# Six of eleven pairs by seven products in the first half's down projection, with one sum of weights made ahead in the MLP's halves

## The chip, the cores and the metric

The kernel runs on one core of a Trainium2 chip. The metric is the device time of one execution in microseconds (us); the figure for a kernel is the median of its runs.

## The reference

One layer of an encoder on 256 tokens of width 2048, in float32:

```python
h = rms_norm(x, attn_norm)
qa, ka, va, qb, kb, vb, ga, gb = split(h @ w_in)
ya = windowed_gqa(qa, ka, va, table, sink)          # 8 heads, 2 key heads, |i-j| <= 128
yb = dilated_attention(qb, kb, vb, table)           # 12 heads in 3 groups of (window, dilation)
merged = sigmoid(ga) * (ya @ w_branch_a) + sigmoid(gb) * (yb @ w_branch_b)
x = x + merged @ w_out
hf = rms_norm(x, ffn_norm)
g = dwconv_centred(hf @ w_ffn_gate, conv_w, conv_b) # width 3, D_FF = 5632
x = x + (gelu(g) * (hf @ w_ffn_up)) @ w_ffn_down
x = x + sigmoid(rms_norm(x, ple_norm) @ w_ple_gate) * (p @ w_ple_proj)
return rms_norm(x, final_norm)
```

The change lies in the down projection (`w_ffn_down`, 5632 x 2048), which is done in two halves of 2816 rows, and in the first product of `w_ple_gate`.

## The kernel before

**Products in three thirds.** A float32 product is made of three matmuls on values that are split into a high and a low part: high by high, high by low, low by high (`thirds`, L363 to L368). So each weight is split on the way: ScalarE (ACT) copies a slice to its high part, `uh` or `vh` (L265), and VectorE (DVE) subtracts that from the slice to get the low part, `ul` or `vl` (L266).

**Pieces, units and rings.** Weights come as pieces of 1 MB (128 x 2048 float32) through SyncE's DMA queue into three `raw` buffers (`load`, L242). `produce` (L248) makes one unit of a piece, 512 or 1024 columns wide, in a ring of six units (`u`) or, for sums of weights, of two (`v`). TensorE (PE) uses units in the order in which they are made.

**Stages.** A: queries, keys, values and attention. B0 to B3: the gates, each followed by the branch projections `ba` and `bb`. D0 and D1: `w_out`, two column halves. E0: gate and up projections of the first half of the MLP, job by job (a job is one block of 128 columns of `w_ffn_gate` or `w_ffn_up`); F00 and F01: the down projection's part that belongs to it, for the two halves of the columns. E1, F10, F11 are the same for the second half. Then pp, G0, G2, G3 (`w_ple_gate`) and the last norm.

**Pairs.** In B, D, F and G0 a piece is a 2 x 2 block of quarters, 512 columns each, that is multiplied by a pair of activation rows (`quad_stage`, L373). A string gives the kind of each pair: `DOWN = "SsSsSsSsSss"` for each F stage. A pair "s" takes eight products (24 matmuls of 128 x 512); a pair "S" takes seven (21 matmuls) of sums, M1 to M7. For that it needs sums of weights, which `produce` makes in place in `raw` on DVE (L258: 1024 columns, L259 and L260: 512 each) ahead of the two `v` units, and sums of activations, which `sums_of` makes (L833). Each product adds up in a PSUM bank of its own, M1 to M7. At the last pair, which is always an "s", the row sums (`row_sums`, L806: L813 on ACT, L814 to L817 on DVE) read M1, M6, M7 and M5, and `residual` (L914) adds all to x (L927, L929). In B the banks M7 and M5 are also used by `bb`, whose last reads are L910.

**What sets the order.** Work of DVE and ACT is attached to places of a stage (`at`, `run_due`); a scheduler then sets the order in each engine's queue, in which an engine works strictly in sequence.

Of the kernel before, what the change touches and what calls it, by code (L numbers as in the profile page):

```python
# [10 lines left out]
F32 = mybir.dt.float32  # L11
# [5 lines left out]
P = 128  # L17
# [78 lines left out]
DOWN = "SsSsSsSsSss"  # L96
# [14 lines left out]
def _pieces():  # L111
# [29 lines left out]
    for half in range(2):  # L141
        names = {"g": "w_ffn_gate", "u": "w_ffn_up"}
        jobs = [(names[kind], f) for kind, f in _ffn(half)]
        joint = 0 if half else JOINT
        e = [(name, k, f) for k in range(KC) for name, f in jobs[:joint]]
        e += [(name, k, f) for name, f in jobs[joint:] for k in range(KC)]
        blocks("E%d" % half, e)
        for s in range(2):
            quads("F%d%d" % (half, s), ("w_ffn_down", 2 * s * WIDE), ("w_ffn_down", (2 * s + 1) * WIDE),
                  DOWN, half * FHALF)  # L150
# [4 lines left out]
    quads("G0", ("w_ple_gate", 0), ("w_ple_gate", WIDE), ALT)  # L155
# [9 lines left out]
def _unit_list():  # L165

    units, of = [], []
    for p, (kind, _) in enumerate(_PIECES):
        if p == 0:
            cuts = [("n", a * P, b * P) for a, b in ((0, 1), (1, 4), (4, 7), (7, 11), (11, PIECE))]  # L170
        elif kind == "S":
            cuts = [("n", 0, WIDE), ("n", 2 * WIDE, 4 * WIDE), ("T13", 0, 2 * WIDE), ("T24", 2 * WIDE, 4 * WIDE)]
        else:
            cuts = [("n", 0, 2 * WIDE), ("n", 2 * WIDE, 4 * WIDE)]
        of.append(list(range(len(units), len(units) + len(cuts))))
        units += [(p, *cut) for cut in cuts]
    return units, of
# [11 lines left out]
def _encoder(ctx: ExitStack, tc, xt, pt, xrow, cols, gainrow, table, onehot, mask, ident_in, wts, out):  # L189
# [22 lines left out]

    flat = big.tile([P, KC + KC * T], F32, name="x", tag="R1")
# [28 lines left out]
    def load(r, a=0, b=PIECE):  # L242
        if a == 0:
            raws[r] = wpool.tile([P, PIECE * P], F32, name="raw", bufs=3)
        nc.sync.dma_start(raws[r][:, a * P:b * P], wts[r][:, a * P:b * P])
        state["raw"] = r + 1

    def produce():  # L248
# [7 lines left out]
        if kind == "T13":  # L256
            q = [raw[:, i * WIDE:(i + 1) * WIDE] for i in range(4)]
            nc.vector.tensor_tensor(raw[:, :2 * WIDE], raw[:, WIDE:3 * WIDE], raw[:, :2 * WIDE], op=ALU.subtract)  # L258
            nc.vector.tensor_tensor(q[2], q[2], q[0], op=ALU.subtract)  # L259
            nc.vector.tensor_tensor(q[3], q[3], q[2], op=ALU.subtract)  # L260
        src = raw[:, a:b]
# [4 lines left out]
        nc.vector.tensor_tensor(lo, src, hi.bitcast(F32), op=ALU.subtract)  # L266
        made[u] = (hi, lo)
# [105 lines left out]
    def quad_stage(stage, moving, combos=None, tags=("M2", "M3", "M4", "P22")):  # L373
# [24 lines left out]
        for i, p in enumerate(pieces):  # L398
            kind = _PIECES[p][0]
            us = _UNITS_OF[p]  # L400
            a, b = moving(2 * i), moving(2 * i + 1)
# [8 lines left out]
            else:  # L410
                s = combos(i)
                sums = [(s[:, 0, e], s[:, 1, e]) for e in range(4)]
                for g, (name, stationary, u, c, gone) in enumerate((
                        ("M1", part(a, 0), 0, 0, 0), ("M7", sums[2], 2, 1, None), ("M5", sums[0], 2, 0, 2),
                        ("M6", sums[1], 3, 0, None), ("M4", part(b, 1), 3, 1, 3),
                        ("M2", part(b, 0), 1, 1, None), ("M3", sums[3], 1, 0, 1))):
# [190 lines left out]

    def view(a, offset, *dims):
        return bass.AP(tensor=a.tensor, offset=a.offset + offset, ap=[a.ap[0], *([step, n] for step, n in dims)])
# [223 lines left out]
    def sums_of(u, tag):  # L833
# [8 lines left out]
        s = tok.tile([P, 2, 4, P], FR, name="S", tag="S%d" % tag)  # L842
# [4 lines left out]
    combos = {}  # L847
# [113 lines left out]
    def activation_row(k):  # L961
        k %= FHALF
        return held["act"][1][k - 16] if 16 <= k < 20 else held["act"][k // 20 * 2][:, k - k // 20 * 20, :]
# [4 lines left out]
    def mlp(kind, n, acc):  # L968
# [21 lines left out]
        else:  # L990
# [8 lines left out]
            m = n % FHALF - 1  # L999
            if 16 <= m < 20:  # L1000
                for i in range(2):
                    halves(activation_row(m + i), u[:, i])
            else:
                i = m // 20 * 2
                d = held["act"][i][:, m - 10 * i:m - 10 * i + 2]
                nc.scalar.activation(d[:, :, :T], u, AF.Copy)
                nc.vector.tensor_tensor(d[:, :, T:], u, d[:, :, :T].bitcast(F32), op=ALU.subtract)
            pair = m // 2
            if DOWN[pair] == "S":
                combos["act", pair] = sums_of(u, pair // 2)  # L1010
# [13 lines left out]

    for half in range(2):
        held["act"] = [big.tile([P, 16, 2 * T], FR, name="act", tag="R1"),
                       [big.tile([P, 2 * T], FR, name="act1", tag="yb%d" % i) for i in range(4)],
                       held["tok"].tile([P, 2, 2 * T], FR, name="act2")]
# [9 lines left out]
        for kind, n in jobs[joint:]:  # L1038
            mlp(kind, n, product(stage, lambda k: hf[:, k, :], KC, "e"))
        if half:  # L1040
# [147 lines left out]
```

## Time and profile before

| | us |
|---|---|
| median of 3 runs | 1457.01 (1456.82 to 1458.02) |
| the profiled execution | 1457.09 |
| its span | 1455.3 |
| PE, DVE, ACT busy | 1444.2, 1196.8, 838.7 |
| B0 to D1, from 310 to 628 of the span | 318.0 |
| E0, 628 to 875.4 | 247.4 |
| F00 and F01, 875.4 to 987.5 | 112.1 |
| E1, 987.5 to 1232.5 | 245.0 |
| F10 and F11, 1232.5 to 1347 | 114.5 |
| pp, G0, G2, G3, end | 108.3 |

Times in the profile count from the start of the span; the granted clock of TensorE was 0.998. PE's rows are pipelined: the time that a row takes in a sequence is the distance to the next start. "PEld" is the loading of weights into TensorE. Behind an instruction stands in brackets how long its engine was idle before it, and what it waited for.

### The profile page before, as it was taken

How to read it: one execution, taken by the hardware profiler on the slowest of the kernel's cores; microseconds unless marked ns; L12 is line 12 of the kernel's file. 1: busy time of each engine (PE TensorE's matmuls, PEld its weight loads, DVE VectorE, ACT ScalarE, POOL GpSimd, SP SyncE). 2: the span in 40 equal slices, each digit the busy share in tenths (PEclk: the TensorE clock that was granted, in tenths of full speed). 3: DMA queues.
4: the chain of work that ended last, by engine and by line, in shares of the span. 5: the costliest groups of instructions: out<-in, count | busy, mean ns of one | idle time of the engine just before them, and what ended most of it. 6: DMA issues, size and time to landing. Idle time of an engine off the chain costs nothing.

```text
span 1455.3 us, 19303 instructions
## 1 busy us (share of the span) xinstructions
PE 1444.2 (99%) x7476; PEld 1234.3 (85%) x7476; DVE 1196.8 (82%) x1626; ACT 838.7 (58%) x1132; POOL 4.8 (0%) x9
## 2 busy tenths in 40 slices
PE   9999999999999999999999999999999999999997
PEld 8888888888888888888888888888888888888785
DVE  7677664679998989988787789987877778999994
ACT  7455544456555656666565565455655656565763
POOL 0000000000000000000000000000000000000000
PEclk9999999999999999999999999999999999999999
DMA  9653445535546456465555545465555554546462
GB/s 336 250 205 145 160 162 178 170 141 203 197 186 236 184 209 231 174 233 201 177 194 184 198 147 225 175 253 187 198 178 199 176 201 173 190 193 235 170 234 85
DMA packets 46455, 282.87 MB, mean 194 GB/s; under 512 B 4948, under 2 KB 9940, under 8 KB 14108
## 3 DMA queue, kind: packets, MB, share of 16 engines
q1 hardware_dynamic: 45644, 280.46, 52.8%
q8 instruction: 58, 0.95, 0.3%
q10 hardware_dynamic: 720, 1.19, 0.2%
q14 instruction: 33, 0.27, 0.1%
HBM read 279.49 MB, written 2.14 MB: 194 GB/s over the span
## 4 chain that ended last, share of the span: by engine, by line
PE 97%; DVE 1%; ACT 1%; issue 0%; DMA 0%; POOL 0%; POOLq 0%; DVEq 0%; SPq 0%; ACTq 0%
PE bank L309 29%; PE bank L316 15%; PE bank L366 14%; PE bank L367 14%; PE bank L368 14%; PE bank L355 2%; PE bank L357 2%; PE bank L293 2%; PE bank L356 2%; PE bank L294 1%; PE bank L861 1%; PE bank L678 0%; PE bank L626 0%; PE bank L625 0%; PE bank L624 0%
## 5 line engine op out<-in xcount | busy, mean ns | idle before, releaser
L265 ACT ACTIVATE uh<-raw 128x1024 fp32r<-128x1024 f32 (+2 forms) x519 | 523.1, 1015 | 394.0 <-PE bank L309 163.8
L266 DVE TENSOR_TENSOR ul<-raw,uh 128x1024 fp32r<-128x1024 f32 (+2 forms) x519 | 594.9, 1166 | 162.6 <-issue 81.0
L309 PE MATMUL bank<-hf,uh 128*128 128x512 f32 x1408 | 336.3, 391 | 0.0
L309 PEld LDWEIGHTS bank<-hf,uh 128*128 128x128 f32 x1408 | 258.9, 188 | 50.1
L316 PEld LDWEIGHTS bank<-hf,ul 128*128 128x128 f32 x1408 | 180.4, 191 | 6.7
L316 PE MATMUL bank<-hf,ul 128*128 128x256 f32 x1408 | 182.8, 283 | 0.0
L265 ACT ACTIVATE vh<-raw 128x1024 fp32r<-128x1024 f32 x92 | 97.0, 1056 | 42.4 <-DVE raw L258 22.9
L266 DVE TENSOR_TENSOR vl<-raw,vh 128x1024 fp32r<-128x1024 f32 x92 | 111.8, 1218 | 0.3
L309 PE MATMUL bank<-hs,uh 128*128 128x512 f32 x432 | 103.6, 392 | 0.0
L447 ACT ACTIVATE t<-bank 128x256 f32<-128x256 f32 x122 | 46.5, 383 | 97.4 <-PE bank L316 86.5
L309 PEld LDWEIGHTS bank<-hs,uh 128*128 128x128 f32 x432 | 79.5, 188 | 15.6
L366 PE MATMUL bank<-uh,act 128*128 128x512 f32 x232 | 90.4, 390 | 0.0
L367 PE MATMUL bank<-ul,act 128*128 128x512 f32 x232 | 90.4, 390 | 0.0
L368 PE MATMUL bank<-uh,act 128*128 128x512 f32 x232 | 90.2, 390 | 0.0
L366 PE MATMUL bank<-uh,hs 128*128 128x512 f32 x172 | 67.3, 391 | 0.0
L368 PE MATMUL bank<-uh,hs 128*128 128x512 f32 x172 | 67.2, 391 | 0.0
L367 PE MATMUL bank<-ul,hs 128*128 128x512 f32 x172 | 67.0, 389 | 0.0
L316 PE MATMUL bank<-hs,ul 128*128 128x256 f32 x432 | 56.6, 284 | 0.0
L258 DVE TENSOR_TENSOR raw<-raw 128x1024 f32<-128x1024 f32 x46 | 56.1, 1220 | 0.5
L316 PEld LDWEIGHTS bank<-hs,ul 128*128 128x128 f32 x432 | 54.5, 191 | 1.0
L367 PE MATMUL bank<-vl,S 128*128 128x512 f32 x138 | 54.0, 392 | 0.1
L366 PE MATMUL bank<-vh,S 128*128 128x512 f32 x138 | 54.1, 398 | 0.0
(242 smaller groups left out, 2229.4 us busy)
## 6 DMA issues: line engine op xcount, KB each, us to landing
raw<-in_wts SPq DMA_DIRECT2D x251, 1024.0 KB, 4.8
raw<-in_wts SPq DMA_DIRECT2D x12, 512.0 KB, 6.7
xr<-in_xrow SPq DMA_DIRECT2D x4, 512.0 KB, 8.2
x<-in_xt SPq DMA_DIRECT2D x13, 128.0 KB, 5.6
hb<-hold SPq DMA_DIRECT2D x3, 514.0 KB, 7.0
hb<-hold SPq DMA_DIRECT2D x2, 768.0 KB, 6.5
last<-in_gainrow SPq DMA_DIRECT2D x1, 1024.0 KB, 8.3
out<-xr SPq DMA_DIRECT2D x4, 256.0 KB, 2.6
```

The lines of the kernel that those rows point to most:

```text
L258: nc.vector.tensor_tensor(raw[:, :2 * WIDE], raw[:, WIDE:3 * WIDE], raw[:, :2 * WIDE], op=ALU.subtract)
L265: nc.scalar.activation(hi, src, AF.Copy)
L266: nc.vector.tensor_tensor(lo, src, hi.bitcast(F32), op=ALU.subtract)
L293: nc.tensor.matmul(acc, hi[:, w], m, start=first, stop=False, skip_group_check=True)
L309: nc.tensor.matmul(acc, weights(u)[0][:, o * P:(o + 1) * P], m, start=first, stop=False, skip_group_check=True)
L316: nc.tensor.matmul(acc[:, T:], weights(u)[1][:, o * P:(o + 1) * P], m[:, :T], start=False, stop=last, skip_group_check=True)
L355: nc.tensor.matmul(acc[:, :n * P], xh, hi, start=(k == 0), stop=False)
L356: nc.tensor.matmul(acc[:, :n * P], xh, lo, start=False, stop=False)
L366: nc.tensor.matmul(acc, sh, wh, start=first, stop=False)
L367: nc.tensor.matmul(acc, sh, wl, start=False, stop=False)
L368: nc.tensor.matmul(acc, sl, wh, start=False, stop=last)
L447: keep(nc.scalar.activation(t, acc[:, T:], AF.Copy, scale=scale))
```

## The change

The strings become `DOWN = ("ZZsZsZsZsZs", "ZsZsZsZsZss")`, one for each half of the MLP, so the first half's stages F00 and F01 have six pairs by seven products where they had five, and the second half's have five as before. G0's four "S" become "Z" as well; B and D keep "S".

A pair "Z" takes seven products as "S" does, in the order M1, M7, M6, M5, M4, M2, M3 and with other signs in its sums. Its quarters come in another order, and of its sums of weights one, q2 - q0 + q1, is made ahead, while the E stage of that half runs: `sum_ahead` loads three quarters' halves (128 x 3 x 256, 384 KB) through SP's queue into a buffer, DVE adds in two steps of 256 columns (L270, L271), and ACT's queue stores the sum (128 KB) in a DRAM tile `ahead`. Two such halves belong to a pair: 24 in all for the first half, 28 for the second with G0. Two buffers take turns ("act2" and "S4"). The load of a "Z" piece then takes 768 KB of weights (L253) and 256 KB of `ahead` (L254); the other two sums are made in place in two ops (L281: 512 columns, L282: 1024). The second of two "Z" in sequence makes its sums after its second unit. The activations of a "Z" pair are kept as the three quarters that M1, M2 and M4 use ("ends") and the four sums, where an "S" kept both whole rows and the sums.

```diff
-DOWN = "SsSsSsSsSss"
+DOWN = ("ZZsZsZsZsZs", "ZsZsZsZsZss")
+LASTS = 30
...
-            pieces.append((c, [(n0, a), (n1, a), (n1, b), (n0, b)]))
+            pieces.append((c, [(n1, a), (n0, a), (n1, b), (n0, b)] if c == "Z" else
+                           [(n0, a), (n1, a), (n1, b), (n0, b)]))
...
-    quads("G0", ("w_ple_gate", 0), ("w_ple_gate", WIDE), ALT)
+    quads("G0", ("w_ple_gate", 0), ("w_ple_gate", WIDE), ALT.replace("S", "Z"))
...
+        elif kind == "Z":
+            cuts = [("n", WIDE, 2 * WIDE), ("n", 2 * WIDE, 4 * WIDE), ("T21", 0, 2 * WIDE), ("T03", 2 * WIDE, 4 * WIDE)]
...
-        nc.sync.dma_start(raws[r][:, a * P:b * P], wts[r][:, a * P:b * P])
+        if _PIECES[r][0] == "Z":
+            nc.sync.dma_start(raws[r][:, WIDE:], wts[r][:, WIDE:])
+            nc.sync.dma_start(raws[r][:, :WIDE], ahead.pop(r))
+        else:
+            nc.sync.dma_start(raws[r][:, a * P:b * P], wts[r][:, a * P:b * P])
...
+    def sum_ahead(p, h, tag):
+        cols = slice(h * T, (h + 1) * T)
+        if h == 0:
+            ahead[p] = dram.tile([P, WIDE], F32, name="ahead%d" % p)
+        q = held["tok"].tile([P, 3, T], F32, name="ahead", tag=tag)
+        nc.sync.dma_start(q, wts[p][:, :3 * WIDE].rearrange("p (q c) -> p q c", c=WIDE)[:, :, cols])
+        def add():
+            nc.vector.tensor_tensor(q[:, 0], q[:, 2], q[:, 0], op=ALU.subtract)
+            nc.vector.tensor_tensor(q[:, 0], q[:, 0], q[:, 1], op=ALU.add)
+        def store():
+            nc.scalar.dma_start(ahead[p][:, cols], q[:, 0])
+        return add, store
+
+    def sums_of_weights(raw):
+        q = [raw[:, i * WIDE:(i + 1) * WIDE] for i in range(4)]
+        nc.vector.tensor_tensor(q[1], q[0], q[1], op=ALU.subtract)
+        nc.vector.tensor_tensor(raw[:, 2 * WIDE:], raw[:, 2 * WIDE:], view(q[0], 0, (0, 2), (1, WIDE)), op=ALU.subtract)
...
+        behind = _PIECES[p][0] == "Z" == _PIECES[p - 1][0]
+        if kind == "T21" and not behind:
+            sums_of_weights(raw)
...
+        if behind and u == _UNITS_OF[p][1]:
+            sums_of_weights(raw)
...
+                if kind == "S":
+                    todo = (("M1", m1, 0, 0, 0), ("M7", sums[2], 2, 1, None), ("M5", sums[0], 2, 0, 2),
+                            ("M6", sums[1], 3, 0, None), ("M4", m4, 3, 1, 3),
+                            ("M2", m2, 1, 1, None), ("M3", sums[3], 1, 0, 1))
+                else:
+                    todo = (("M1", m1, 0, 0, 0), ("M7", sums[2], 2, 1, None), ("M6", sums[1], 2, 0, 2),
+                            ("M5", sums[0], 3, 0, None), ("M4", m4, 3, 1, 3),
+                            ("M2", m2, 1, 1, None), ("M3", sums[3], 1, 0, 1))
...
+            x, y = place
+            for b, k, t0, t1 in ((0, 0, 0, P), (1, 1, 0, T)):
+                o = x[:, :, b:b + (t1 - t0) // P]
+                v = u[:, k, t0:t1].rearrange("p (b t) -> p b t", t=P)
+                nc.scalar.activation(o[:, 0], v, AF.Copy)
+                nc.vector.tensor_tensor(o[:, 1], v, o[:, 0].bitcast(F32), op=ALU.subtract)
+            combos["act", pair] = sums_of(u, None, y)
...
+        todo = [(p, h) for p in sevens(half) for h in range(2)]
+        for i, (kind, n) in enumerate(jobs[joint:]):
+            if len(stores) > 1:
+                stores.pop(0)()
+            for f in adds:
+                at((stage, 8), f)
+            del adds[:]
+            def ask():
+                if todo and i > 1 and (i % 2 == 0 or i < LASTS):
+                    add, store = sum_ahead(*todo.pop(0), ("act2", "S4")[i % 2])
+                    adds.append(add)
+                    stores.append(store)
+                else:
+                    stores.append(lambda: None)
+            at((stage, 9), ask)
             mlp(kind, n, product(stage, lambda k: hf[:, k, :], KC, "e"))
```

The scheduler moves some of this. On DVE the ten sums of the first half that use the "act2" buffer stand in B1 to D1 instead of E0. At the start of B2, where `bb` has just ended (L910 before, L956 now, reads its banks), DVE's rows before:

```order
L266 TENSOR_TENSOR vl_3913<-raw_3782,vh_3912 128x1024
L266 TENSOR_TENSOR ul_3947<-raw_3847,uh_3946 128x1024
L910 SCALAR_TENSOR_TENSOR c_3810<-c_3810,bank_3952 128x512
L912 TENSOR_TENSOR c_3810<-c_3810 128x512
L266 TENSOR_TENSOR ul_3975<-raw_3889,uh_3974 128x512
L910 SCALAR_TENSOR_TENSOR c_3811<-c_3811,bank_3953 128x512
L266 TENSOR_TENSOR ul_3985<-raw_3889,uh_3984 128x1024
```

and now, with an add in it:

```order
L305 TENSOR_TENSOR vl_3913<-raw_3782,vh_3912 128x1024
L305 TENSOR_TENSOR ul_3947<-raw_3847,uh_3946 128x1024
L956 SCALAR_TENSOR_TENSOR c_3810<-c_3810,bank_3952 128x512
L270 TENSOR_TENSOR ahead_6350<-ahead_6350 128x256
L305 TENSOR_TENSOR ul_3975<-raw_3889,uh_3974 128x512
L958 TENSOR_TENSOR c_3810<-c_3810 128x512
L956 SCALAR_TENSOR_TENSOR c_3811<-c_3811,bank_3953 128x512
L305 TENSOR_TENSOR ul_3985<-raw_3889,uh_3984 128x1024
```

One add of 256 columns stands between the two reads of `bb`'s banks.

At the border from F00 to F01 the rows of DVE before are these (`raw_8211` is F01's first pair, `c` the row sums, `xr` is x):

```order
L816 TENSOR_TENSOR c_8337<-bank_7957,c_8337 128x512
L266 TENSOR_TENSOR ul_8289<-raw_8211,uh_8288 128x1024
L266 TENSOR_TENSOR vl_8296<-raw_8211,vh_8295 128x1024
L259 TENSOR_TENSOR raw_8211<-raw_8211 128x512
L817 TENSOR_TENSOR c_8338<-bank_7957,c_8338 128x512
L260 TENSOR_TENSOR raw_8211<-raw_8211 128x512
L266 TENSOR_TENSOR ul_8330<-raw_8251,uh_8329 128x1024
L266 TENSOR_TENSOR ul_8334<-raw_8251,uh_8333 128x1024
L266 TENSOR_TENSOR vl_8300<-raw_8211,vh_8299 128x1024
L927 TENSOR_TENSOR xr_4918<-xr_4918,bank_7986 128x512
```

and now (`raw_8369` and `raw_8405` are F01's first and second pair, both "Z"; L859 to L862 are the row sums, L281 and L282 the sums of weights):

```order
L305 TENSOR_TENSOR vl_8478<-raw_8369,vh_8477 128x1024
L305 TENSOR_TENSOR ul_8495<-raw_8405,uh_8494 128x1024
L859 TENSOR_TENSOR c_8500<-bank_8102,c_8500 128x512
L282 TENSOR_TENSOR raw_8405<-raw_8405 128x1024
L860 TENSOR_TENSOR c_8501<-bank_8098,c_8500 128x512
L973 TENSOR_TENSOR xr_4918<-xr_4918,bank_8139 128x512
L861 TENSOR_TENSOR c_8500<-bank_8110,c_8500 128x512
L862 TENSOR_TENSOR c_8501<-bank_8110,c_8501 128x512
L973 TENSOR_TENSOR xr_4918<-xr_4918,bank_8143 128x512
L973 TENSOR_TENSOR xr_4918<-xr_4918,bank_8114 128x512
L975 TENSOR_TENSOR xr_4918<-xr_4918,c_8500 128x1024
L973 TENSOR_TENSOR xr_4918<-xr_4918,bank_8210 128x512
```

The row sums, which stood among the sums of the first pair, now stand behind the low parts of the first pair and around the second sum of the second.

PE's rows of F01's second "Z" now (`ends` and `S` are its activations, L407, L408 and L409 the three thirds):

```order
L407 MATMUL bank_8537<-uh_8484,ends_6211 128x512
L408 MATMUL bank_8537<-ul_8485,ends_6211 128x512
L409 MATMUL bank_8537<-uh_8484,ends_6211 128x512
L407 MATMUL bank_8541<-vh_8549,S_6212 128x512
L407 MATMUL bank_8545<-vh_8549,S_6212 128x512
L407 MATMUL bank_8582<-uh_8494,ends_6211 128x512
L408 MATMUL bank_8582<-ul_8495,ends_6211 128x512
L407 MATMUL bank_8553<-vh_8561,S_6212 128x512
L407 MATMUL bank_8557<-vh_8561,ends_6211 128x512
L409 MATMUL bank_8582<-uh_8494,ends_6211 128x512
L408 MATMUL bank_8541<-vl_8550,S_6212 128x512
L409 MATMUL bank_8541<-vh_8549,S_6212 128x512
```

The products with the high parts `vh` stand ahead of those with the low parts `vl` of the same units.

In E1, DVE's rows of one stretch before:

```order
L266 TENSOR_TENSOR ul_10069<-raw_9972,uh_10068 128x1024
L266 TENSOR_TENSOR ul_10081<-raw_9972,uh_10080 128x1024
L451 TENSOR_TENSOR gw_9990<-bank_10041,t_10084 128x256
L977 TENSOR_TENSOR gw_9990<-gw_9990,rms_5811 128x512
L981 SCALAR_TENSOR_TENSOR gw_9990<-gw_9990,cl_73 128x255
L983 SCALAR_TENSOR_TENSOR gw_9990<-gw_9990,cl_73 128x255
L981 SCALAR_TENSOR_TENSOR gw_9990<-gw_9990,cl_73 128x255
L266 TENSOR_TENSOR ul_10126<-raw_10019,uh_10125 128x1024
L983 SCALAR_TENSOR_TENSOR gw_9990<-gw_9990,cl_73 128x255
```

and now:

```order
L305 TENSOR_TENSOR ul_10129<-raw_10021,uh_10128 128x1024
L305 TENSOR_TENSOR ul_10141<-raw_10021,uh_10140 128x1024
L499 TENSOR_TENSOR gw_10039<-bank_10096,t_10144 128x256
L271 TENSOR_TENSOR ahead_10295<-ahead_10295 128x256
L1049 TENSOR_TENSOR gw_10039<-gw_10039,rms_5806 128x512
L270 TENSOR_TENSOR ahead_10348<-ahead_10348 128x256
L1053 SCALAR_TENSOR_TENSOR gw_10039<-gw_10039,cl_73 128x255
L271 TENSOR_TENSOR ahead_10348<-ahead_10348 128x256
L1055 SCALAR_TENSOR_TENSOR gw_10039<-gw_10039,cl_73 128x255
L1053 SCALAR_TENSOR_TENSOR gw_10039<-gw_10039,cl_73 128x255
L305 TENSOR_TENSOR ul_10191<-raw_10073,uh_10190 128x1024
```

Between the rows of the gate's convolution stand the two adds of one sum, and the second add of another.

More of the change, by code (lines that the diff above doesn't have):

```diff
@@ L412, in quad_stage @@
                 sums = [(s[:, 0, e], s[:, 1, e]) for e in range(4)]
[L413 to L416, printed above, removed]
+                m1, m2, m4 = (part(a, 0), part(b, 0), part(b, 1)) if (stage, i) not in ends else ends[stage, i]
+                if kind == "S":
[6 more added lines that the diff above has]
+                            ("M2", m2, 1, 1, None), ("M3", sums[3], 1, 0, 1))
+                for g, (name, stationary, u, c, gone) in enumerate(todo):
                     run_due(stage, i, g)
```

79 lines of the change are left out of this document (55 added, 24 removed).

## The prediction

> **What bounds the kernel now.** I read the page's busy times and chain first, then the table of stretches, then PE's own waits, and only then DVE's and ACT's.
>
> ```profile
> PE 1444.2 (99%) x7476; PEld 1234.3 (85%) x7476; DVE 1196.8 (82%) x1626; ACT 838.7 (58%) x1132; POOL 4.8 (0%) x9
> PE 97%; DVE 1%; ACT 1%; issue 0%; DMA 0%; POOL 0%; POOLq 0%; DVEq 0%; SPq 0%; ACTq 0%
> PE bank L226 <- DVE mhalf L221: 1.1, 1, 1.1
> PE bank L293 <- ACT uh L265: 0.2, 1, 0.2
> ```
>
> The chain that ended last is PE for 97% of the span, and the list of PE's waits holds 1.3 us. So an instruction less on PE is time won, and one less elsewhere is not, except where DVE is nearly as full as PE. The stretches show where that is (columns: window, length, busy time of PE, PEld, DVE, ACT, POOL, granted clock, DMA share, GB/s):
>
> ```profile
> 310.00:628.00 318.00, 317.99 (x1430) 261.05 (x1429) 299.38 (x370) 189.19 (x219) 0.00 (x0) 1.00 0.53 198
> 628.00:875.40 247.40, 247.40 (x1429) 218.55 (x1427) 195.24 (x289) 149.56 (x210) 0.71 (x1) 1.00 0.53 188
> 875.40:930.90 55.50, 55.50 (x246) 45.92 (x245) 51.96 (x58) 30.20 (x33) 0.00 (x0) 1.00 0.53 196
> 930.90:987.50 56.60, 56.60 (x251) 46.89 (x250) 50.92 (x55) 29.60 (x32) 0.00 (x0) 1.00 0.59 225
> 987.50:1232.50 245.00, 245.00 (x1411) 216.54 (x1410) 188.88 (x272) 144.09 (x196) 0.00 (x0) 1.00 0.52 186
> 1232.50:1347.00 114.50, 114.50 (x511) 94.42 (x510) 109.76 (x132) 66.38 (x79) 0.00 (x0) 1.00 0.57 211
> ```
>
> These are B0 to D1, E0, F00, F01, E1, and F10 with F11. In B to D and in the F stages DVE is busy for 90 to 96% of the time; in the E stages for 77 to 79%.
>
> **Step 1: two more pairs by seven products.** PE loses one product, three matmuls, in F00 and in F01. What a matmul costs in a row is the distance of starts, not its busy time:
>
> ```profile
> 931.60 0.39 PE L366 MATMUL bank<-vh,S 128*128 128x512 f32 x1
> 931.82 0.39 PE L367 MATMUL bank<-vl,S 128*128 128x512 f32 x1
> 932.05 0.39 PE L368 MATMUL bank<-vh,S 128*128 128x512 f32 x1
> 932.28 0.39 PE L366 MATMUL bank<-vh,S 128*128 128x512 f32 x1
> 932.96 0.39 PE L366 MATMUL bank<-vh,S 128*128 128x512 f32 x1
> ```
>
> Three matmuls take 0.68 us (931.60 to 932.28), so the six are 1.36 us: **-1.36**. A pair of eight products is 8 x 0.68 = 5.44 us on PE, one of seven 4.76.
>
> **Step 2: DVE in the pairs.** These rows price its work (columns: busy us, mean ns; starts follow 0.08 us less apart than that, as 424.85, 425.45 below show):
>
> ```profile
> L266 DVE TENSOR_TENSOR vl<-raw,vh 128x1024 fp32r<-128x1024 f32 x92 | 111.8, 1218 | 0.3
> L258 DVE TENSOR_TENSOR raw<-raw 128x1024 f32<-128x1024 f32 x46 | 56.1, 1220 | 0.5
> L266 DVE TENSOR_TENSOR ul<-raw,uh 128x512 fp32r<-128x512 f32 x47 | 32.3, 687 | 10.6 <-ACT uh L265 10.3
> L259 DVE TENSOR_TENSOR raw<-raw 128x512 f32<-128x512 f32 x46 | 31.5, 685 | 0.3
> L260 DVE TENSOR_TENSOR raw<-raw 128x512 f32<-128x512 f32 x46 | 31.5, 684 | 0.2
> L451 DVE TENSOR_TENSOR pair<-bank,t 128x256 f32<-128x256 f32 x44 | 18.4, 418 | 0.2 <-ACT t L447 0.2
> ```
>
> S made three sums of weights in place, 1.22 + 0.69 + 0.68 = 2.59 us; Z makes two (512 and 1024 wide), 1.90: 0.69 less a pair. A pair of eight products has two lo halves (2.44 us); a Z has one of 512 and three of 1024 (4.34) besides its sums, so it costs DVE 6.24, 3.8 more than "s". F00 and F01: 5 x -0.69 + 3.8 = +0.4 us of DVE each while PE gets 0.68 less, so DVE goes from 51.96 of 55.5 to about 52.4 of 54.8. F10 and F11 save 3.4 each, G0 2.8. None of this is on the path by itself, but two places in F have less cover.
>
> (a) F00 and F01 begin with two Z: 2 x 6.24 = 12.5 us of DVE against 9.5 of PE. The 3.0 us must be made ahead; the new PE order helps, since it does the second Z's hi products before its lo ones. I take 0; the other end is half the deficit, +1.5, if the ring of two v units keeps DVE from going ahead.
>
> (b) The border from F00 to F01. The last three products' banks are read by the row sums (L813 to L817), and F01's M7 and M5 need those banks:
>
> ```profile
> 924.46 0.68 DVE L259 TENSOR_TENSOR raw<-raw 128x512 f32<-128x512 f32 x1
> 925.06 0.68 DVE L817 TENSOR_TENSOR c<-bank,c 128x512 f32<-128x512 f32 x1
> ```
>
> The last row sum ends at 925.74, and M5 starts at 932.96 (the last row of the fence before): 7.2 us to spare, because two pairs "ss" end the stage. Now one "s" does, 5.44 us less: 1.8 us are left, and the new order sets the row sums behind the first Z's lo halves and among the second Z's sums. The sums start only after ACT's copy of M1 and behind two 1024 ops (2.28 us by start distance). 2.28 - 1.8 = about +0.5 us of wait: taken **+0.5**, ends 0 (they follow at once) and +2.5 (both ops and the 1024 sum of the second Z, 1.22, and a row sum, 0.68, all late). It replaces no wait that was there.
>
> **Step 3: sums made ahead.** 24 times for half 0 and 28 for half 1: a load of 384 KB on SP, two DVE ops of 256 columns (0.84 us), a store of 128 KB from ACT's queue, and later 256 KB of each Z's megabyte come from that store. In E this has cover:
>
> ```profile
> L266 DVE TENSOR_TENSOR ul<-raw,uh 128x1024 fp32r<-128x1024 f32 x87 | 104.3, 1221 | 42.8 <-issue 40.9 <-PE bank L316 1.9
> 701.93 3.65 PE bank L309 x16
> 705.59 1.91 PE bank L316 x16
> ```
>
> The first row is DVE's lo halves in E1 alone: DVE stood idle for 42.8 us before them, nearly all of it with a full ring of units ahead of PE. The adds of E1 are 28 x 0.84 = 23.4 us, so 19 us of slack remain; E0 gets the 14 that are not moved forward, 11.7 us. The other two rows are the chain in an E job: 3.65 + 1.91 = 5.56 us, two units of the ring of six, so a full ring is two jobs ahead, 11.1 us; a DVE that falls a microsecond or two behind inside a job is not seen by PE. I take 0. Price if the cover goes: in Rival 1.
>
> Ten of half 0's sums stand earlier, in B1 to D1, where DVE is the second bound: 10 x 0.84 = 8.4 us against 318.0 - 299.38 = 18.6 us of idle DVE. There the order matters; PE waits for DVE at the start of a B stage:
>
> ```profile
> 424.85 0.68 DVE L266 TENSOR_TENSOR ul<-raw,uh 128x512 fp32r<-128x512 f32 x1
> 425.45 0.68 DVE L910 SCALAR_TENSOR_TENSOR c<-c,bank 128x512 f32<-128x512 f32 x1
> 426.18 0.19 PEld L366 LDWEIGHTS bank<-vh,S 128*128 128x128 f32 x1 [0.26 <-DVE c L910]
> 607.84 0.19 PEld L366 LDWEIGHTS bank<-vh,S 128*128 128x128 f32 x1 [0.42 <-ACT vh L265]
> 620.53 0.19 PEld L367 LDWEIGHTS bank<-vl,S 128*128 128x128 f32 x1 [0.27 <-DVE vl L266]
> 1349.02 0.42 PEld L861 LDWEIGHTS bank<-ident,xr 128*128 128x128 f32 x4 [0.42 <-DVE xr L927]
> 1374.05 0.19 PEld L367 LDWEIGHTS bank<-vl,S 128*128 128x128 f32 x1 [0.51 <-DVE vl L266]
> ```
>
> At 426.18 PE waits for L910, DVE's last read of the bank that M5 takes over. An add of 0.42 us, 0.34 by start distance, now stands two ops before it, and likewise at the starts of B3 and D0. If nothing else moved that is 3 x 0.34 = +1.0; but the order now has other PE work ahead of M5 (transposes and products with ready weights, some 0.5 us), which covers most. Taken +0.2 for the three (0 to +1.0). D1 has two more waits (607.84 and 620.53); three adds in it and a new order on both engines: from -0.4 (both gone) to +1.3 (three times 0.42), taken 0, since the adds stand where DVE waits for ACT. E0's beginning needs D1's last work from DVE, up to 1.7 us (four adds) later; E0's first column blocks do not need it, so I take +0.1, with +1.0 as the far end. At 1374.05 in G0 PE waits 0.51 us from the end of one weight load to the next, of which some 0.25 is lost (a row's distance is 0.23); G0's sums are shorter by 0.69, so **-0.25**. At 1349.02, at F11's end, PE waits for DVE's last row of x (0.42); F11's DVE has less to do, but that row depends on the last product, so 0.
>
> **DMA.** The new transfers by their nearest rows (columns: KB, us to landing):
>
> ```profile
> raw<-in_wts SPq DMA_DIRECT2D x251, 1024.0 KB, 4.8
> raw<-in_wts SPq DMA_DIRECT2D x12, 512.0 KB, 6.7
> raw<-in_wts SPq DMA_DIRECT2D x1, 320.0 KB, 5.1
> xr<-in_xrow SPq DMA_DIRECT2D x4, 512.0 KB, 8.2
> out<-xr ACTq DMA_DIRECT2D x4, 256.0 KB, 2.9
> x<-in_xt ACTq DMA_DIRECT2D x1, 136.0 KB, 2.5
> ```
>
> A buffer of the sums is turned once in two jobs, 11.1 us: load 5.1, adds 0.84, store 2.5, together 8.4; with the slowest row, 8.2 + 0.84 + 2.9 = 11.9. At 5.1 nothing waits, and 5.1 is the row of nearest size. Traffic in E goes from 188 GB/s by 0.52 MB in 5.56 us, 94, to some 282, and DMA's share of 0.53 rises with it to about 0.8, so transfers get slower, which is Rival 1's ground. A Z's load is 768 + 256 KB where it was 1024; SP's queue has one more issue, and three raw buffers stand behind it: 0.
>
> The Trainium skill, page "DMA: Bandwidth & Descriptors", section "Anatomy of one DMA", gives a fixed 2.0 us and 436 KB per us beyond that; as an estimate from it the load of 384 KB would take 2.9 us and the store 2.3, a turn would be 6.0 us, and the sum would stay as it is. The same page, section "Bandwidth", has the rule to batch transfers to at least 1 MiB, which speaks against the change; the trace's 2.5 us for 136 KB lies near that estimate, while 5.1 us for 320 KB lies well above the 2.8 us that it would give.
>
> **Sum:** -1.36 + 0 + 0.5 + 0.2 + 0 + 0.1 - 0.25 = -0.8. The profiled execution took 1457.09 us (span 1455.3 and 1.8 around it), 0.08 above the median of the runs, 1457.01. So I forecast 1456.2, 0.06% less, which a measurement of this kernel can't tell from no change (some 0.2%, 2.9 us). With the ends of all terms: (a) +1.5, (b) 0 to +2.5, B starts 0 to +1.0, D1 -0.4 to +1.3, E0 0 to +1.0; a few of them together give 1455 to 1458.5.
>
> **Rivals.**
> 1. Slower: the turn of the sums' buffers limits E. Place: SP's queue in E1, where each 384 KB load stands ahead of a weight load and waits until the store from two jobs before has landed. It decides from a turn of over 11.1 us; at 11.9 each turn loses 0.8 us, half 1 has 14 turns of each buffer, 11 us, and with more traffic it would be more. The 11.1 us of the ring take the first part. For it speak DMA's share of 0.8 and the 8.2 us row, against it the 5.1 us row and that three raw buffers are loaded behind. Time: +4 to +10, 1461 to 1467. Chance 0.14.
> 2. The F stages become DVE's: at the "ZZ" starts and the border the ends of (a) twice and (b) come together, 3.0 + 2.5 - 1.36 - 0.35 = +3.8, or half of it. For it speaks 96% of DVE, against it the PE order that puts ready products first. 1457.5 to 1460.9. Chance 0.14.
> 3. Faster: DVE's relief takes PE's small waits away as well, G0's 0.25, D1's 1.0, the B starts' 0.3, F11's 0.4, and no new ones come: -1.36 - 1.95 = -3.3, 1453.7. For it: new orders everywhere. Against: the adds lie in just those stages. Chance 0.09.
> 4. It changes nothing at all, since another limit holds F: 1457.0. Against it stands PE's 55.50 of 55.50. It is not told from my forecast by the time, only by F's length; chance 0.03.
>
> The forecast has the remaining 0.60, with 1455.0 to 1457.8 as its own range. Faster by over 0.2% (below 1454.1) is most of Rival 3: 0.08. Slower (above 1459.9) is Rival 1 and a fifth of Rival 2: 0.17. The rest, 0.75, is within 0.2%. Left out are 0.07 below 1454.0 and about 0.12 above 1461.0.
>
> **What the profile after would show.** Step 1: six matmuls fewer on PE, F00 and F01 each 0.5 to 0.7 us shorter. (a) and (b): a wait of PE for DVE at the first M7 or M5 of F01, under 1 us. Step 3: E0 and E1 as long as before (247.4 and 245.0) with DVE 10 and 22 us fuller; longer E stages with SP waiting for the stores would make Rival 1 right. B2 to D0: waits for L956 (L910 now) of 0.1 to 0.4 us. I am wrong if E grows by more than a microsecond, or if F shrinks by more than 1.4.

## The result, and the profile after

The changed kernel takes 1474.2 us (median of 6 runs, 1472.93 to 1482.97) against 1456.95 (6 runs, 1456.75 to 1458.02): a ratio of 1.0128, 95% interval 1.0103 to 1.0152. It is 1.3% slower, where the forecast was 1456.2. The profiled execution has a span of 1475.0 us, 19.7 longer than before. Its page, in the lines that answer to those shown of before:

```profile
PE 1450.7 (98%) x7470; PEld 1236.7 (84%) x7470; DVE 1220.0 (83%) x1730; ACT 828.1 (56%) x1148; POOL 5.0 (0%) x9
PE 83%; DMA 7%; DVE 7%; issue 2%; ACT 1%; SPq 0%; POOLq 0%; POOL 0%; DVEq 0%; ACTq 0%
PE bank L350 23%; PE bank L407 12%; PE bank L409 12%; PE bank L408 12%; PE bank L357 12%; DMA ahead<-in_wts 4%; DVE ul L305 3%; DMA ahead<-ahead 3%; PE bank L396 2%; PE bank L398 2%; PE bank L397 2%; PE bank L334 2%; PE bank L335 1%; DMA raw<-in_wts 1%; PE bank L907 1%
```

PE has its six instructions less (7470 for 7476), but the chain that ended last is PE for only 83% of the span. Two transfers that did not exist before are in it by name: the load of a sum (`ahead<-in_wts`) and its store (`ahead<-ahead`). The stretches, cut where each stage begins on PE, show where (columns as before; B0 to D1, E0, F00 with F01, E1, the rest):

```profile
310.00:630.40 320.40, 318.60 (x1428) 260.69 (x1428) 304.88 (x391) 187.72 (x219) 0.00 (x0) 1.00 0.58 213
630.40:877.60 247.20, 247.20 (x1427) 218.33 (x1426) 202.69 (x322) 143.63 (x215) 0.81 (x1) 1.00 0.60 219
877.60:989.70 112.10, 112.10 (x494) 91.99 (x493) 104.25 (x114) 63.40 (x70) 0.00 (x0) 1.00 0.57 211
989.70:1253.10 263.40, 251.87 (x1410) 219.15 (x1410) 206.87 (x334) 137.57 (x201) 0.00 (x0) 0.99 0.65 230
1253.10:1475.00 221.90, 212.32 (x952) 175.06 (x950) 189.63 (x246) 127.79 (x175) 2.93 (x3) 0.98 0.51 186
```

Measured from the first matmul of each stage to that of the next, in both kernels:

| stage | before | after | difference |
|---|---|---|---|
| to the start of E0 | 627.24 | 630.40 | +3.16 |
| E0 | 247.10 | 247.20 | +0.10 |
| F00, F01 | 113.02 | 112.11 | -0.91 |
| E1 | 244.90 | 263.35 | +18.45 |
| F10 to the end | 223.04 | 221.98 | -1.06 |
| span | 1455.30 | 1475.04 | +19.74 |

So all but 3 us of the loss is in E1. The waits of E1, by engine, tell what PE stood behind (columns: us in total, times, longest):

```profile
PE bank L357 <- DVE ul L305: 11.1, 10, 3.2
DVE ahead L270 <- DMA ahead<-in_wts: 41.4, 14, 5.2
SPq L267 <- DMA ahead<-ahead: 108.8, 18, 10.4
```

PE waits for the low parts of weights; DVE, which makes them, stands at the first add of a sum (L270) 14 times and for 41.4 us until the sum's load has landed; and that load (L267) stands in SP's queue until the store of the sum that used the buffer before has landed. The chain of E1 between 1064 and 1083 us follows this back (columns: start, us, what):

```profile
1064.25 6.46 DMA ahead<-ahead
...
1070.76 2.91 DMA ahead<-in_wts
...
1073.76 0.43 DVE ahead L270
1074.19 0.10 DVE ahead L271
...
1074.55 4.55 DMA ahead<-ahead
...
1079.15 3.20 DMA ahead<-in_wts
```

A store takes 6.5 or 4.6 us, a load 2.9 or 3.2, and nothing lies between them but an add. The chain goes from one buffer to the other: the add that starts at 1073.76 belongs to one sum, and the second add of the sum before it, whose store starts at 1074.55, stands behind it in DVE's queue. DVE's rows at this place show both things, in the order in which DVE has them:

```profile
1069.16 0.41 DVE L270 TENSOR_TENSOR ahead<-ahead 128x256 f32<-128x256 f32 x1
1073.76 0.43 DVE L270 TENSOR_TENSOR ahead<-ahead 128x256 f32<-128x256 f32 x1 [4.20 <-DMA ahead<-in_wts]
1074.10 0.75 DVE L271 TENSOR_TENSOR ahead<-ahead 128x256 f32<-128x256 f32 x2
1074.77 2.35 DVE L305 TENSOR_TENSOR ul<-raw,uh 128x1024 fp32r<-128x1024 f32 x2
1077.04 0.42 DVE L499 TENSOR_TENSOR pair<-bank,t 128x256 f32<-128x256 f32 x1
1082.47 0.42 DVE L270 TENSOR_TENSOR ahead<-ahead 128x256 f32<-128x256 f32 x1 [5.01 <-DMA ahead<-in_wts]
```

The first two rows are the first adds of two sums, one in each buffer; the third row has the second adds of both; the last row is the next sum of the first buffer. Between the last add of the first sum and that row lie some 3 us of DVE's work, but a store and a load must pass there, some 8 us. DVE works in order, so it waits.

When PE's starts are set beside those of before, the first 67 us of E1 (to 1056) lose 0.1 us, although DVE waits 14.2 us for sums' loads in them. Then it loses 9.0 by 1093, 6.5 between 1111 and 1137, and 2.9 between 1148 and 1175, in steps. This fits a ring of units that stands full ahead of PE, pays for the first waits, and is empty after them.

Not all of the 18.45 us is waiting. Two stretches of 3.4 us each, within 2 us of the end of two of PE's longest waits, have a granted clock of 0.50 (columns as before):

```profile
1085.80:1089.10 3.30, 3.30 (x12) 2.81 (x11) 2.97 (x8) 2.30 (x4) 0.00 (x0) 0.50 0.79 276
1130.10:1133.40 3.30, 3.30 (x17) 3.24 (x16) 1.04 (x2) 3.12 (x5) 0.00 (x0) 0.50 0.48 160
```

In them PE's matmuls of 512 columns start 0.43 us apart, where 0.23 is their usual distance. These stretches cost 3.1 us of the 18.45, and the waits the other 15.3. Of the twelve profiles of this document, those of the changed kernel and of runs (2), (4) and (6) below have such stretches before the last 30 us; they are also the only ones in which, from 60 to 1440 us, two starts on PE lie 2.0 us or more apart. Run (1), with at most 1.4 us, has none. The six runs of the changed kernel have mean clocks of 0.992 to 0.997, and the longest of them has the lowest. So in these runs the lower clock goes with long waits of PE and adds to their price; what sets the limit was not tried.

### The profile page after: what moved, and what is told of

It reads as the page before. It is cut to its first block, busy times and chain, and to the rows that moved or that the text cites. A ratio compares the mean times of both kernels' runs of the same rounds, so it can differ in the third digit from the quotient of the medians.

```text
span 1475.0 us, 19731 instructions
## 1 busy us (share of the span) xinstructions
PE 1450.7 (98%) x7470; PEld 1236.7 (84%) x7470; DVE 1220.0 (83%) x1730; ACT 828.1 (56%) x1148; POOL 5.0 (0%) x9
## 4 chain that ended last, share of the span: by engine, by line
PE 83%; DMA 7%; DVE 7%; issue 2%; ACT 1%; SPq 0%; POOLq 0%; POOL 0%; DVEq 0%; ACTq 0%
PE bank L350 23%; PE bank L407 12%; PE bank L409 12%; PE bank L408 12%; PE bank L357 12%; DMA ahead<-in_wts 4%; DVE ul L305 3%; DMA ahead<-ahead 3%; PE bank L396 2%; PE bank L398 2%; PE bank L397 2%; PE bank L334 2%; PE bank L335 1%; DMA raw<-in_wts 1%; PE bank L907 1%
## 5 line engine op out<-in xcount | busy, mean ns | idle before, releaser
L357 PE MATMUL bank<-hf,ul 128*128 128x256 f32 x1408 | 187.3, 285 | 11.5 <-DVE ul L305 11.1
L304 ACT ACTIVATE vh<-raw 128x1024 fp32r<-128x1024 f32 x96 | 100.8, 1057 | 62.1 <-DVE raw L281 25.0
L305 DVE TENSOR_TENSOR vl<-raw,vh 128x1024 fp32r<-128x1024 f32 x96 | 116.1, 1218 | 0.9
L409 PE MATMUL bank<-uh,act 128*128 128x512 f32 x218 | 84.9, 390 | 0.0
L408 PE MATMUL bank<-ul,act 128*128 128x512 f32 x218 | 84.8, 389 | 0.0
L407 PE MATMUL bank<-uh,act 128*128 128x512 f32 x218 | 84.6, 389 | 0.0
L270 DVE TENSOR_TENSOR ahead<-ahead 128x256 f32<-128x256 f32 x52 | 21.8, 420 | 73.2 <-DMA ahead<-in_wts 69.2
L407 PE MATMUL bank<-uh,hs 128*128 128x512 f32 x172 | 67.4, 392 | 0.0
L408 PE MATMUL bank<-ul,hs 128*128 128x512 f32 x172 | 67.1, 390 | 0.0
L409 PE MATMUL bank<-uh,hs 128*128 128x512 f32 x172 | 67.0, 390 | 0.0
L408 PEld LDWEIGHTS bank<-ul,act 128*128 128x128 f32 x218 | 40.9, 188 | 8.6
L409 PEld LDWEIGHTS bank<-uh,act 128*128 128x128 f32 x218 | 40.9, 188 | 8.5
```

The source lines that it names most:

```text
L304: nc.scalar.activation(hi, src, AF.Copy)
L357: nc.tensor.matmul(acc[:, T:], weights(u)[1][:, o * P:(o + 1) * P], m[:, :T], start=False, stop=last, skip_group_check=True)
L407: nc.tensor.matmul(acc, sh, wh, start=first, stop=False)
L408: nc.tensor.matmul(acc, sh, wl, start=False, stop=False)
L409: nc.tensor.matmul(acc, sl, wh, start=False, stop=last)
```

## The experiments

Each starts from the changed kernel. Theory "order": the scheduler's dense rows on DVE. "Turn": two buffers are too few at any order. "Queue": SP, waiting for stores, holds the weights back. "Traffic": the added bytes. "Work": the added DVE time. E1's lengths below are from first matmul to first matmul, as in the table. Where no ratio is given, the kernel was run once.

**Adds tied to their place (1).** `keep` ties an instruction behind what the program put before it on its engine.

```diff
-            nc.vector.tensor_tensor(q[:, 0], q[:, 2], q[:, 0], op=ALU.subtract)
-            nc.vector.tensor_tensor(q[:, 0], q[:, 0], q[:, 1], op=ALU.add)
+            keep(nc.vector.tensor_tensor(q[:, 0], q[:, 2], q[:, 0], op=ALU.subtract))
+            keep(nc.vector.tensor_tensor(q[:, 0], q[:, 0], q[:, 1], op=ALU.add))
```

> The two adds of every sum are tied to their place in the program (step 8 of the next job), so that DVE's queue holds one sum in every job, 5.56 us apart, and none of the first half's in B1 to D1; loads, stores and the two buffers stay. In the changed kernel E1 takes 263.4 us (244.9 before) and B1 to D1 about 2.7 us more than before. Theory 'order': the loss in E1 comes from DVE's queue, where the scheduler put the next add of a buffer five rows (3 to 4 us) behind the store that must land and be followed by a load, some 8 us. Then E1 falls to 245 to 248 and B1 to D1 to within 0.5 us of before, and the whole is 1455 to 1459. Theory 'turn': the two buffers' turn of load, adds and store is longer than two jobs, 11.1 us, in any order. Then E1 stays over 255. Theory 'queue': SP, which waits for the stores, holds back the weights' loads; then E1 also stays over 255.

Measured: 1461.27 us, ratio 1.0036 (1.0022 to 1.0050); E1 248.97, E0 starts at 627.77. The same instructions, buffers and transfers in another order on DVE take back 14.4 of the 18.45 us of E1 (the 3.1 us of half clock among them) and 2.6 of the 3.16 before E0. E1 still loses 4.1 us, a little more than "order" allowed, and the same wait is left, smaller:

```profile
DVE ahead L270 <- DMA ahead<-in_wts: 25.8, 9, 5.2
```

**Four buffers, order left to the scheduler (2).** The sums use the four buffers of the `v` units, which E leaves free.

```diff
-        q = held["tok"].tile([P, 3, T], F32, name="ahead", tag=tag)
+        q = held["tok"].tile([P, 3, T], F32, name="ahead", tag=tag, bufs=2)
...
-                    add, store = sum_ahead(*todo.pop(0), ("act2", "S4")[i % 2])
+                    add, store = sum_ahead(*todo.pop(0), ("vh", "vl")[i % 2])
```

> The sums use four buffers (those of the two v units, which the E stages leave free) in place of two; the scheduler's order of the adds stays bunched. Theories 'order' and 'turn' both: a load is issued two jobs earlier, so DVE does not wait for it, and E1 falls to 245 to 250; these buffers are not free in B1 to D1, so nothing is moved there and these lose the 2.7 us. Whole 1455 to 1460. Theory 'queue': SP waits as little, so E1 falls too. Theory 'traffic' (the added 0.5 MB a job slow the weights): E1 stays over 255.

Measured: 1474.43 us, E1 255.72, E0 255.43, E0 starts at 627.39. My expectation missed: E1 falls by only 7.6, and E0 now loses 8.3. The stretches of E0 and of E1:

```profile
627.40:882.80 255.40, 251.29 (x1427) 220.86 (x1426) 209.19 (x342) 145.09 (x215) 0.81 (x1) 0.99 0.65 232
994.95:1250.70 255.75, 248.97 (x1410) 217.61 (x1409) 205.69 (x332) 139.70 (x201) 0.00 (x0) 0.99 0.67 235
```

With more buffers the scheduler took the loads as early as they were free and set the adds denser: E1's 28 sums were loaded between 987 and 1101 us, one every 4.2 us, where the changed kernel loaded its last at 1167. So room that buffers give is used up by the order, and "turn" alone does not explain E1. It also bears on B0 to D1: with buffers that are not free there, nothing is moved there, and E0 starts 0.15 us after that of the kernel before.

**The adds alone (3).** The second half's sums are neither loaded (but the first two) nor stored, and its pairs load their weights as they lie, so this kernel leaves that part of the computation out.

```diff
+        if second and tag in kept:
+            q = kept[tag]
+        else:
+            ...
...
-            nc.scalar.dma_start(ahead[p][:, cols], q[:, 0])
+            if not second:
+                nc.scalar.dma_start(ahead[p][:, cols], q[:, 0])
```

> In the second half only the adds are left: of its sums, the first two are loaded, no other is loaded and none is stored, and the pairs' loads take the megabyte of weights as it lies (this part of the computation is left out). DVE does the same 56 adds in E1. Theories 'order', 'turn', 'queue', 'traffic': E1 falls to 245 to 246, whole about 1456 to 1458, since the work itself fits DVE's idle time. Theory 'work' (the adds fill DVE): E1 stays over 255.

Measured: 1456.19 us, E1 244.90. "Work" falls: E1 has its 56 adds and is as long as before.

**Loads and stores without the adds (4).** The adds of the second half are left out.

```diff
         def add():
+            if p >= _STAGES["F10"][0]:
+                return
```

> In the second half the loads and stores of the sums are left and the 56 adds are taken out (the stored tile is the first quarter, so this part of the computation is left out). DVE has nothing to wait for; SP still waits for the stores of two jobs before, and the traffic is the same. Theory 'order' (DVE's waits in its queue): E1 falls to 245 to 248, whole 1456 to 1460. Theories 'queue' and 'traffic': E1 stays over 255.

Measured: 1471.4 us, E1 259.00. That spoke for "queue" and "traffic", but the experiment was badly made: without the adds the store waits for the load itself, on ACT's queue, and ACT then stands where DVE stood:

```profile
ACT uh L306 <- DMA ahead<-in_wts: 21.1, 7, 4.4
...
ACT t L497 <- DMA ahead<-in_wts: 12.6, 5, 2.8
ACT ends L1087 <- DMA ahead<-in_wts: 8.8, 2, 4.8
```

It shows only that the chain of store and load stalls whichever engine meets it in its queue. Traffic was tried by itself in (8).

**Tied and four buffers (5).** The edits of (1) and (2) together.

> Adds tied to their place and four buffers together. Alone, tying left E1 at 249.0 us, and four buffers alone left E1 at 255.7 and made E0 longer by 8.3, since the scheduler then took the loads earlier and set the adds as densely as the buffers allowed. Theory 'chain' (a sum's load, adds and store follow each other through memory, some 9 to 12 us a turn, and whichever queue meets it in order stalls when adds stand closer than that): with one sum a job and 22 us between two uses of a buffer nothing waits, E0 247.1, E1 245 to 246, F as in the changed kernel, whole 1455.0 to 1456.5, at or just below the kernel before. Theory 'traffic': E1 stays at 249 or more.

Measured: 1455.49 us, ratio 0.9989 (0.9980 to 0.9997): faster than both kernels, by 0.11% against the one before. E1 244.91, F00 and F01 112.08, E0 247.67, start of E0 627.27. E1's stretch:

```profile
987.00:1231.90 244.90, 244.90 (x1409) 216.51 (x1408) 207.63 (x333) 143.16 (x201) 0.00 (x0) 1.00 0.68 245
```

and what SP waited for longest in it:

```profile
SPq L267 <- DMA ahead<-ahead: 94.6, 16, 10.3
```

No wait of DVE for a sum's load is listed in E1 any more. SP still waits 94.6 us for stores, nearly as long as in the changed kernel, at a higher rate of transfer (245 GB/s against 230), and PE loses nothing. So neither SP's wait nor the traffic is the price; what costs is a wait in the queue of the engine that makes the weights' parts.

**Tied, two buffers, transfers from GpSimd's queue (6).** Besides the edit of (1):

```diff
-        nc.sync.dma_start(q, wts[p]...)   # the rest of the line is cut here
+        nc.gpsimd.dma_start(q, wts[p]...)
...
-            nc.scalar.dma_start(ahead[p][:, cols], q[:, 0])
+            nc.gpsimd.dma_start(ahead[p][:, cols], q[:, 0])
```

> Adds tied to their place, two buffers, and the sums' loads and stores are issued from GpSimd's queue, which has nothing else to do, so that neither SP (weights) nor ACT (high parts) waits for them. Tied alone, E1 was 249.0 and SP still waited 107 us for stores. Theory 'queue' (SP's waits hold the weights back): E1 245 to 246. Theory 'chain': the turn of two buffers stays, DVE still waits for loads, E1 247 to 250.

Measured: 1496.81 us, E0 266.47, E1 267.14: a miss, and the worst of all. Three successive transfers of that queue (in brackets: idle before, and what it waited for):

```profile
1030.22 0.75 POOL L267 DMA_DIRECT2D ahead<-in_wts  x1 [2.88 <-DMA ahead<-ahead]
1031.23 0.59 POOL L274 DMA_DIRECT2D ahead<-ahead  x1 [0.25 <-issue]
1036.72 0.74 POOL L267 DMA_DIRECT2D ahead<-in_wts  x1 [4.91 <-DMA ahead<-ahead]
```

In one queue, a store stands behind a load that waits for the other buffer's store to land, so the two buffers take turns one after the other instead of side by side. On two queues, SP and ACT, they overlap. The share of this in the loss is not shown by itself: the loads also took longer to land than in (1) (4.5 us against 3.2, medians of 52), the stores less (3.6 against 4.5), and PE has the granted clock of 0.50 in four stretches with 23.9 us in all before the last 30 us.

**Tied, four buffers, GpSimd's queue (7).** The edits of (5) and (6).

> All three: adds tied to their place, four buffers, loads and stores from GpSimd's queue. Theory 'chain': as with four buffers tied, 1455.0 to 1456.5, since nothing waits there any more. Theory 'queue': this one is faster than four buffers tied by the rest that SP's waits cost, 1 to 4 us.

Measured: 1455.36 us, ratio 0.9987 (0.9977 to 0.9996); E0 247.09, E1 244.90. With four buffers the one queue costs nothing, though its loads land only after 5.6 us, and against (5) it gains nothing that this can measure. "Queue" falls.

**The traffic alone (8).** Every load and store of the second half is made, but the stores write a tile that was loaded once, nobody reads the loads, and the second half's adds are left out.

```diff
         def add():
+            if second:
+                return
...
-            nc.scalar.dma_start(ahead[p][:, cols], q[:, 0])
+            nc.scalar.dma_start(ahead[p][:, cols], (kept[0] if second else q)[:, 0])
```

> In the second half every load and every store of a sum is still issued, but they do not depend on each other: the loads are read by nobody, the stores write one tile that was loaded at the start, and the adds are left out (so this part of the computation is left out). The traffic is the changed kernel's, and denser. Theory 'traffic': E1 stays over 255. Theories 'chain' and 'queue': E1 244.9 to 246.

Measured: 1456.16 us, E1 244.90. "Traffic" falls: the same bytes, free of each other and at 248 GB/s in E1, cost nothing.

**Half the sums, tied (9) and free (10).** 14 sums in the second half, asked for in every second job, with the changed kernel's two buffers; (9) also has the edit of (1). The other seven pairs take their weights as they lie, so that part of the computation is left out.

```diff
-        todo = [(p, h) for p in sevens(half) for h in range(2)]
+        todo = [(p, h) for p in sevens(half) for h in range(2)][:14 if half else None]
...
-                if todo and i > 1 and (i % 2 == 0 or i < LASTS):
-                    add, store = sum_ahead(*todo.pop(0), ("act2", "S4")[i % 2])
+                if todo and i > 1 and (i % 2 == 0 or (i < LASTS and not half)):
+                    add, store = sum_ahead(*todo.pop(0), ("act2", "S4")[i // 2 % 2 if half else i % 2])
```

> The changed kernel's two buffers and queues, adds tied to their place, but in the second half only 14 of the 28 sums are made, one in every second job, so that a buffer is used again after 22 us and not after 11 (the other seven pairs take the weights as they lie; this part of the computation is left out). With 28 sums tied E1 was 249.0. Theory 'chain': a turn of load, adds and store has room in 22 us, so E1 is 244.9 to 245.5, with two buffers. Theory 'a second buffer pair is needed' (four buffers helped for another reason than time, for example by taking the waits off SP's queue): E1 is 246 to 248.

Measured: 1455.71 us, E1 244.91. Two buffers are enough when a buffer comes round every 22 us instead of 11; DVE has no wait for a sum's load.

> The same 14 sums, asked for in every second job, but with the order left to the scheduler, which sets them in the first half of E1's rows, as close as the 28 stand in the changed kernel. Theory 'chain with the order': E1 loses about what the changed kernel lost over its first 14 sums, after the reserve of the ring was used up: 2 to 8 us, 247 to 253. Theory 'rate' (what counts is how many sums E1 holds): E1 as with the tied ones, 244.9 to 245.5.

Measured: 1457.15 us, E1 244.91. My expectation missed, and the reason is instructive. The scheduler did set the 14 sums as densely as in the changed kernel, and DVE did wait for loads in E1:

```profile
DVE ahead L270 <- DMA ahead<-in_wts: 20.0, 7, 4.4
```

20.0 us of waits cost E1 nothing. The last of these sums was done by 1071 us; in the changed kernel DVE had waited 18.4 us by 1059 us, PE lost its first time at 1061, and more than half of the sums were still to come. This fits waits that are harmless until they have used up the ring's reserve, and was not tested further.

## Why the prediction was wrong

The step that failed is step 3, "I take 0", for the sums in E. It had two supports. The first, that DVE has the time (23.4 us of adds against 42.8 us of idle), was right: (3) shows 0. The second, that a buffer's turn (load 5.1, adds 0.84, store 2.5, together 8.4 us) fits in two jobs of 11.1 and "a DVE that falls a microsecond or two behind inside a job is not seen by PE", was wrong in what it left out. I took one sum per job, as the program asks for them. The queue has four in a burst (first adds at 1098.1, 1099.1, 1107.6 and 1111.7 us, the next only at 1121.8), and in a burst a buffer's next add stands some 3 us behind its last. The rows for that were at hand: the order that I showed for E1 has adds of two sums interleaved in a few rows, and I did not price the distance between two uses of one buffer. (1) shows that the order is most of it: 14.4 of 18.45 us. The sign that the prediction gave for being wrong, an E stage longer by more than a microsecond, is what came.

The price of a turn's parts was off both ways, and the sum happened to be right. Measured in the changed kernel, by the medians of all 52 sums, with a row that was there before:

```profile
ahead<-in_wts SPq DMA_DIRECT2D x52, 384.0 KB, 3.2
ahead<-ahead ACTq DMA_DIRECT2D x52, 128.0 KB, 4.5
out<-xr ACTq DMA_DIRECT2D x4, 256.0 KB, 2.9
```

The load takes 3.2 us, not 5.1, and the store 4.5, not 2.5: I had priced a store into memory by a row that loads into the chip's buffers. The third row, which stores into memory, would not have told either. With the adds, the medians make 8.5. What is left of 11.1 is 2.6 us, and tied adds with two buffers still lose 4.1 us in E1 (1). Single turns there are longer than the medians, and (9), with twice the time for each turn, loses nothing. The chain that ended last in (1) has these two pairs of a store and the load behind it, near where E1 begins to lose:

```profile
1128.38 6.80 DMA ahead<-ahead
1135.26 3.28 DMA ahead<-in_wts
...
1153.44 3.18 DMA ahead<-ahead
1156.68 6.64 DMA ahead<-in_wts
```

They take 10.1 and 9.8 us, and with the adds and their place in DVE's queue the first of these turns is 12.1 us, from store to store. What makes one transfer land in 3.2 us and another in 6.8 was not tried. The traffic that I forecast for E, 282 GB/s and a DMA share of 0.8, was too high: E1 has 230 and 0.65.

The Trainium skill, page "DMA: Bandwidth & Descriptors", section "Anatomy of one DMA", says that most of the fixed cost is waiting for the receipt of the write, and that this is slowest where the write goes to HBM. The trace does not settle this: 4.5 us for 128 KB into DRAM stand beside 3.2 us for three times as much out of it, but the last stores of the same trace, 256 KB into DRAM, took 2.9 us. The section's formula, which it gives for transfers that GpSimd issues while these are issued by SP and ACT, gave as an estimate 2.3 us for the store and 2.9 for the load; with GpSimd as the issuer, (7) measured 4.5 and 5.6. The measurement decides.

Rival 1, with a chance of 0.14, had the right stage and the right buffers, and its wait in the wrong queue. It has SP's queue hold back the weights; but in (5) SP waits 94.6 us for stores and E1 loses nothing. So the sign given for it, "longer E stages with SP waiting for the stores", came, but SP's waiting was not the cause; what costs is DVE's wait for the load. Its size, 1461 to 1467 from a turn of 11.9 us, fits (1), where the turn is all that is left: 1461.27. It says nothing of the order, and the changed kernel's 1474.2 lies above it. By its own words it decides "from a turn of over 11.1 us"; in the changed kernel loads of one buffer followed each other in 7.7 to 20.0 us where E1 lost time.

The other steps, by the stages:

- Step 1 and (b): forecast -1.36 + 0.5 = -0.86 in F00 and F01; measured -0.91, and -0.89 to -0.96 in all others but (9), which has -0.53 for a reason that was not looked for. The six matmuls gain what was said. The 0.45 that came off lies in five small gaps between PE's starts, 0.21 us at F00's start (880.0 and 880.3), 0.17 at the border (934.4 and 934.7) and 0.10 at 940.5, so the border is only a part, and (a), which I took as 0, is as much.
- B1 to D1: forecast +0.2, with E0's beginning +0.1; measured +3.16. Part of it is the same chain: SP waited 38.6 us for stores in this stretch, and in D1 ACT waits for weights that SP has not fetched, and PE for ACT:

```profile
581.44 2.01 ACT L304 ACTIVATE uh<-raw 128x1024 fp32r<-128x1024 f32 x2 [3.10 <-DMA raw<-in_wts]
586.75 0.19 PEld L407 LDWEIGHTS bank<-vh,S 128*128 128x128 f32 x1 [1.40 <-ACT uh L304]
```

  I had counted the adds moved there, and not the loads and stores that move with them. Another 0.5 us is no cost of the change: PE is that much behind at 25 us already, and up to 310 us all engines have the same instructions in the same order as before. So it is in (1), whose 0.53 us this explains. E0 began at 627.65 to 630.40 us in the five profiles with that order (the changed kernel, 3, 4, 8 and 10), and at 627.27 to 627.77 in the six without (1, 2, 5, 6, 7, 9). In the first group PE, DVE and SP have the same instructions in the same order up to E0, and ACT has them with one neighbouring pair exchanged at most; so the size, 0.4 to 3.2 us, differs from execution to execution, and what sets it was not tried.
- E0: forecast 0, measured +0.10. Only 14 of its 24 sums stood in it; with all 24 in it and a dense order it loses 8.3 us (2).
- G0 and F1: forecast -0.25, measured -1.06 from F10 to the end. PE's gap at 1374.05, with the start after it, is gone (0.35), and about 0.5 us is won between F11 and pp, which the forecast put at 0.

Taken together, the steps outside the chain were worth about -1.7 us, as (5) and (7) show, where the forecast had -0.8.

## What to carry to other kernels

When a step passes through memory and back through a few buffers, count the distance between two uses of one buffer in the queue of each engine that waits, not the rate at which the program asks for it: the scheduler's order here, with two buffers and with four, went as fast as the buffers came free. Whichever engine waits for such a transfer in order stops all that is queued behind it, so tie that wait to where the data will have landed, and give it buffers enough; either alone was not enough here. And idle time of an engine is cover for added work; a wait that stands in front of work is covered only as long as the work made ahead lasts. Where the waits reach PE, look at the granted clock behind them as well: it added 3.1 us here.

## What the runs showed that I had not expected

A store of 128 KB into DRAM took 4.5 us to land, longer than a load of 384 KB (3.2), beside the same stream of weights. More buffers alone made E0 8.3 us longer. And moving a two-buffer chain to an otherwise idle queue made the kernel 35 us slower than on two busy ones (1496.81 against 1461.27).
